# Attention weights of two heads side by side, retention decays moved to the values and the output, a third pair of banks in the last projection

## The chip, the cores and the metric

The kernel runs on one core of a Trainium2 chip. The metric is the device time of one execution in microseconds (us); the median of three executions of the kernel before is 3140.94 us (3136.82 to 3141.93). Below, PE is the matrix engine, DVE the vector engine, ACT the scalar engine, POOL the general engine, SP the queue that issues the DMAs.

## What is computed

Two layers of a block with four token mixers side by side, on 2048 tokens of width 1024 and 256 context tokens: a gated linear recurrence, a delta-rule memory (GDN), retention, and attention in a window. The change touches retention and attention. Cut to them:

```python
def retention_chunked(q, k, v, log_gamma, s0, with_out):   # per head, chunk by chunk
    s_new = s * c_dec + einsum('cd,ce->de', k_i * k_dec, v_i)
    att = einsum('id,jd->ij', q_i, k_i) * dmat
    o = einsum('cd,de->ce', q_i * q_dec, s) + einsum('ij,je->ie', att, v_i)

# attention: softmax over 256 context keys and a window of three blocks of 128 keys, then
#   y = P @ v, two query heads to each of two key-value heads, times a gate

y = concatenate([ya, yb, yr, yd]) @ w_out      # the projection at the end of each layer
x = x + gate * rmsnorm(y)
```

Retention runs forward and backward, so each decay exists for two directions.

## The kernel before

Tokens are cut into 18 tiles of 128 (two of context) and 9 blocks of two tiles. Each layer runs four stages:

- **A**: norms, and the projections for the recurrence and GDN.
- **B**: `ret_tile` and `gdn_tile` for every tile, with the projection for retention beside them as filler; the two scans `ret_scan` and `gdn_chain` begin here.
- **C**: the projection for attention, `swa_prep` and `swa_tile` (attention), and `ret_out` and `gdn_out`, which join what stage B left in DRAM with the scanned states.
- **D**: the projection with `w_out` (`proj`) and the norm and residual (`post`). In layer 0 it also prepares the next layer; in layer 1 (the **last projection**) it ends the program.

Python generators yield pieces of work, `weave` interleaves them, and this decides which PSUM buffer each piece takes. PSUM has eight banks of 128x512 f32: two `pd`, two `pg`, two `pm`, and `sc`, which is two banks in one tile. After that `Plan` lists the instructions with their dependencies, and sets a new order on every engine by the length of the chain behind each instruction, with a price for changes of shape on PE. So any edit moves instructions everywhere, but a bank is handed on in the order in which the program asked for it.

An f32 product stands in the trace as two MATMUL records, so four products show as x8. The products of the large projections are in f32r and show as one record each, and so do transposes.

The places of the change:

- `ret_tile` (stage B) per tile: q and k are rotated; `kd` holds k times the key decay of both directions (DVE); four products of `kd` (128 columns as weights) with 64 columns of v give the state increments `KV` (L145, tile `sc<-G`, 128x64). `qd` holds q times the query decay of both directions (POOL); four transposes turn q and k (L787), four more turn `qd` (L793), ACT copies both, and `qdT` goes to DRAM as `Qr`.
- `ret_scan`: the state S, forward in partitions 0 to 63 and backward in 64 to 127.
- `ret_out` (stage C) per tile: four products of `Qr` (128x128 weights) with 64 columns of S in one `pm` bank (L145, `pm<-U` 128\*128, 128x64), one DVE addition (L853), then the norm of each head.
- `swa_tile` (stage C): for each of four head steps the scores go to `sc`, the softmax runs on DVE and ACT, the weights are transposed in `pg` (L1470) and copied to `sPT` (ACT, L1471). After the second step of each half, the product with the values: for each of up to five key tiles two products, one for each key-value head, each with 64 columns of v as weights and 128 columns of `sPT`, into the two halves of a `pm` bank (`pm<-U` 128\*64, 128x128); then the gate (DVE, L1479). There are two such groups per tile.
- `proj` in the last projection: tile s = 0 of a block goes to the two `pd` banks, tile s = 1 to the two `pg` banks, 48 products of 512 columns each. `post` squares both banks on ACT (L1558), sums (L1560), takes the inverse root on POOL (L330) and scales both banks on DVE (L1571); a bank is free after its L1571. The input of a block (`h`) has two buffers, loaded and split by ACT, DVE and POOL (L1520 to L1524).

Of the kernel before, what the change touches and what calls it, by code (L numbers as in the profile page):

```python
# [16 lines left out]
NT = 18  # L17
# [6 lines left out]
PMAP = dict(x.split(":") for x in "ptk:0 ptv:h1 pt:0 pu:1 ptq:1 pm0:0 pm1:1 pc0:h0 pc1:h1 po:1 p3:1 rkv:h0 rpt:0 rpt2:0 rpo:h0 ch:h0".split())  # L24
# [45 lines left out]
    "C": ([("sqk", 384, 1), ("sks", 384, 1), ("srope", 256, 2), ("rota", 256, 1), ("rotb", 256, 1), ("sVc", 128, 2), ("sV", 128, 5),  # L70
           ("sqs", 512, 1), ("szt", 512, 1), ("szl", 512, 1), ("shs", 512, 1), ("roq", 512, 1), ("goq", 512, 1), ("goS", 512, 1),
           ("roS", 256, 1), ("roo", 256, 1), ("roz", 256, 1), ("rosq", 256, 1), ("goo", 256, 1), ("gosq", 256, 1), ("goz", 256, 1),
           ("roy", 256, 1), ("goy", 256, 1), ("sy", 256, 2), ("sPT", 640, 2), ("szb", 512, 2), ("sP", 640, 2)],
# [51 lines left out]
class Net:  # L125
# [134 lines left out]
    def setup(self):  # L260
# [33 lines left out]
        self.Qr = self.t(dp, [NT, 128, 512], "Qrd")  # L294
        self.KV = self.t(dp, [NT, 128, 256], "KVd")
        self.Sr = self.t(dp, [NT, 128, 256], "Srd")
# [411 lines left out]
    def ret_setup(self, sp):  # L708
# [20 lines left out]
        self.cdec = self.t(self.lp, [128, 4], "rcd")  # L729
        for d in range(2):  # L730
            nc.vector.tensor_scalar(self.qdec[:, :, d], lg[:, 4 * d:4 * d + 4], io[:, 2 * d:2 * d + 1], None, op0=MULT)
            nc.vector.tensor_scalar(self.kdec[:, :, d], lg[:, 4 * d:4 * d + 4], io[:, 2 * d + 1:2 * d + 2], None, op0=MULT)
            nc.vector.tensor_scalar(self.cdec[64 * d:64 * d + 64], lg[64 * d:64 * d + 64, 4 * d:4 * d + 4], 128.0, None, op0=MULT)
# [13 lines left out]
    def ret_tile(self, t, pa, pb, pp):  # L747

        nc = self.nc
# [18 lines left out]
        kd = self.t(pp, [128, 4, 2, 64], "rdd")  # L768
        nc.vector.tensor_tensor(kd, qk[:, 256:].rearrange("p (h e) -> p h e", h=4)[:, :, None].to_broadcast([128, 4, 2, 64]),
# [8 lines left out]
        self.st('K').dma_start(self.KV[t], kv)  # L778
# [35 lines left out]
    def ret_scan(self, lo, hi):  # L814
        nc = self.nc
        if lo == 0:
            self.rS = self.t(self.lp, [128, 4, 64], "rS", bufs=2)
            nc.vector.memset(self.rS, 0.0)
        fl = lambda a: a.rearrange("p h e -> p (h e)")
        for i in range(lo, hi):  # L820
# [3 lines left out]
            self.st('S').dma_start(self.Sr[tf, 0:64], fl(S)[0:64])  # L824
            self.st('S').dma_start(self.Sr[tb, 64:128], fl(S)[64:128])
# [3 lines left out]
            kv = self.t(self.lp, [128, 4, 64], "rsk", bufs=2)  # L829
            nc.sync.dma_start(fl(kv)[0:64], self.KV[tf, 0:64])  # L830
            nc.sync.dma_start(fl(kv)[64:128], self.KV[tb, 64:128])
            S2 = self.t(self.lp, [128, 4, 64], "rS", bufs=2)
            nc.vector.tensor_tensor(S2, S, self.cdec[:, :, None].to_broadcast([128, 4, 64]), op=MULT)
# [4 lines left out]
    def ret_out(self, t, pp):  # L838
# [3 lines left out]
        q = self.t(pp, [128, 512], "roq")  # L842
        nc.sync.dma_start(q, self.Qr[t])
        S = self.t(pp, [128, 256], "roS")
        nc.sync.dma_start(S, self.Sr[t])
# [578 lines left out]
    def swa_tile(self, t, qT, zb, pp):  # L1424
# [14 lines left out]
        y = self.t(pp, [128, 2, 128], "sy", bufs=2)  # L1439
# [23 lines left out]
        def second(hh, g):  # L1463
            p = P[hh, g]
            pT = PT[g] = self.t(pp, [128, 640], "sPT", bufs=2)
            for a in range(0, nk, 512):
# [4 lines left out]
                nc.scalar.copy(pT[:, a:a + w], pt[:, :w])  # L1471
# [8 lines left out]
            if hh:  # L1480
                self.st('s').dma_start(self.yT[t // 2, :, 6:8, s * 128:(s + 1) * 128], y)
            yield 1.3, 0
# [4 lines left out]
    def pass_d(self, pp):  # L1487
# [40 lines left out]
        outs = [0]  # L1528
# [512 lines left out]
```

## Time and profile before

| | us |
|---|---|
| median of three runs | 3140.94 |
| the profiled execution | 3140.24 |
| its span in the trace | 3138.5 |
| stage B of layer 0 and of layer 1, about | 400 to 960, 1990 to 2540 |
| stage C of layer 0 and of layer 1, about | 960 to 1400, 2540 to 2916 |
| last projection | 2916 to 3125 |
| after the last product | 3125 to 3138 |

In the trace's views a row of the timeline is a run of equal instructions: its start, its length up to the end of the last one, the engine, the line, the operation, the tile written and the tiles read, and how many. The time from one row's start to the next row's start is what the run took of PE's queue; the length itself also holds the time in which the last result runs out of the array, beside which the next run has begun. A bracket at a row's end gives the idle time ahead of it and what ended it.

### The profile page before, as it was taken

To read this page: it belongs to the slowest core of one execution; us is meant where nothing else is said; L and a number is where in the kernel's file an instruction comes from. 1 tells how busy PE (TensorE), PEld (TensorE's weight loads), DVE (VectorE), ACT (ScalarE), POOL (GpSimd) and SP (SyncE) were. 2 spreads that over 40 slices of the span, in tenths; PEclk is the share of its full clock that TensorE was granted. 3 is DMA by queue.
4 is the path that set the end of the run, shared out by engine and by line. 5 is a ranking of instruction groups with operands and counts; after the bars stand their busy time and mean duration, and the time that the engine had idled before them with its cause. 6 is when DMAs were issued, how large, how long until landed. Compare 5 with 4: busy or idle time off the path is not lost. (4 is left out here: it accounts for less than half of the span.)

```text
span 3138.5 us, 78206 instructions
## 1 busy us (share of the span) xinstructions
PE 2940.4 (94%) x31820; PEld 2497.3 (80%) x31820; DVE 1938.9 (62%) x4258; ACT 1334.3 (43%) x2930; POOL 1220.2 (39%) x1197
## 2 busy tenths in 40 slices
PE   4999979999999999979999998899999899999987
PEld 3999867778877888867789998678878688888766
DVE  4587777676665576653255787767666456767321
ACT  3466644444443344442134666444444424445211
POOL 2133345555542232334352333456555422323332
PEclk8999989999999999999999999999999999999998
DMA  7243465554456655375652435556444664544431
GB/s 275 95 173 134 166 168 150 167 153 118 134 180 187 199 163 162 122 264 196 197 202 106 162 144 162 161 150 176 141 140 120 220 198 139 171 152 142 153 122 68
DMA packets 410121, 504.69 MB, mean 161 GB/s; under 512 B 94056, under 2 KB 311560, under 8 KB 403104
## 3 DMA queue, kind: packets, MB, share of 16 engines
q1 hardware_dynamic: 409760, 499.68, 49.7%
q8 instruction: 250, 4.10, 0.5%
q14 instruction: 111, 0.91, 0.1%
HBM read 320.06 MB, written 179.50 MB: 159 GB/s over the span
## 5 line engine op out<-in xcount | busy, mean ns | idle before, releaser
L145 PE MATMUL pd<-w,h 128*128 128x512 f32 (+1 forms) x3408 | 984.4, 411 | 26.2 <-DVE U L1560 16.1
L145 PEld LDWEIGHTS pd<-w,h 128*128 128x128 f32 x3408 | 613.4, 192 | 158.6 <-ACT U L1558 18.5
L145 PE MATMUL pd<-h,w 128*128 128x256 f32 x3360 | 589.2, 294 | 1.1 <-DVE U L479 1.1
L145 PEld LDWEIGHTS pd<-h,w 128*128 128x128 f32 x3360 | 479.8, 193 | 10.6 <-issue 5.0
L330 POOL TENSOR_TENSOR U<-U,mh 128x4 f32<-128x4 f32 (+2 forms) x174 | 179.5, 1034 | 379.6 <-DVE U L329 361.2
L145 PE MATMUL pg<-h,w 128*128 128x256 f32 x1680 | 294.3, 294 | 4.7 <-DVE U L1571 3.6
L145 PE MATMUL pm<-U 128*64 128x128 f32 (+4 forms) x3280 | 249.4, 274 | 26.4 <-ACT U L1089 7.7
L145 PEld LDWEIGHTS pg<-h,w 128*128 128x128 f32 x1680 | 245.0, 191 | 9.9 <-DVE U L1571 3.8
L145 PEld LDWEIGHTS pm<-U 128*64 128x64 f32 (+2 forms) x3280 | 197.6, 143 | 68.4 <-issue 22.3
L145 PE MATMUL pg<-w,h 128*128 128x512 f32 x816 | 228.6, 394 | 1.3 <-DVE U L1571 1.3
L145 PEld LDWEIGHTS <-U 64*64 64x64 f16 x6512 | 153.2, 109 | 55.1 <-issue 45.4
L145 PE MATMUL pg<-U 64*64 64x64 f16 x6512 | 188.4, 195 | 1.2 <-DVE U L1031 1.1
L145 PEld LDWEIGHTS pg<-w,h 128*128 128x128 f32 x816 | 154.4, 190 | 38.8 <-issue 3.3
L1031 DVE TENSOR_TENSOR U<-pg,C 128x512 f16<-128x512 f32 x180 | 122.0, 684 | 64.3 <-PE pg L145 63.5
L625 DVE SCALAR_TENSOR_TENSOR U<-U 128x256 f32<-128x256 f32 x318 | 159.8, 552 | 1.1 <-POOL U L558 1.1
L1560 DVE TENSOR_TENSOR U<-U 128x1 f32<-128x1 f32 x34 | 7.7, 230 | 234.9 <-ACT U L1558 234.9
L1456 ACT ACTIVATE U<-sc,U 128x640 f32<-128x640 f32 (+2 forms) x136 | 104.2, 766 | 103.7 <-DVE U L1454 88.5
L1471 ACT COPY U<-pg 128x512 f32<-128x512 f32 (+2 forms) x248 | 100.7, 436 | 103.6 <-PE pg L1470 50.1
L1558 ACT ACTIVATE U<-pd 128x512 f32<-128x512 f32 x34 | 20.0, 594 | 276.7 <-PE pd L145 164.4
L1453 DVE TENSOR_REDUCE U<-sc 128x1 f32<-128x640 f32 (+2 forms) x136 | 106.2, 781 | 47.3 <-PE sc L145 45.7
L1046 DVE STREAM_TRANSPOSE U<-U 128x512 f16<-128x512 f16 x144 | 100.8, 703 | 45.8 <-ACT U L1042 45.3
L1042 ACT CAST U<-pg 128x512 f16<-128x512 f32 x144 | 84.0, 588 | 82.9 <-PE pg L145 77.9
(297 smaller groups left out, 6038.3 us busy)
## 6 DMA issues: line engine op xcount, KB each, us to landing
hTd<-h SPq DMA_DIRECT2D x18, 2048.0 KB, 6.7
h<-hTd SPq DMA_DIRECT2D x72, 512.0 KB, 5.6
h<-hTd SPq DMA_DIRECT2D x18, 2048.0 KB, 9.8
MCd<-U SPq DMA_DIRECT2D x72, 256.0 KB, 3.3
cMC<-MCd SPq DMA_DIRECT2D x140, 128.0 KB, 3.3
U<-yTd SPq DMA_DIRECT2D x34, 512.0 KB, 4.5
U<-in_w_in_dram SPq DMA_DIRECT2D x58, 256.0 KB, 3.9
hgd<-U SPq DMA_DIRECT2D x53, 256.0 KB, 2.5
```

The source lines that it names most:

```text
L145: self.nc.tensor.matmul(out, lhsT, rhs, start=start, stop=stop)
L330: nc.gpsimd.tensor_tensor(out, out, self.mh[:, :n], op=ALU.pow)
L625: nc.vector.scalar_tensor_tensor(z[:, i], xb[:, f, j:j + 256], cw[:, f, j:j + 1], z[:, i], op0=MULT, op1=ADD)
L1031: nc.vector.tensor_tensor(M, p1, lev(k), op=MULT)
L1042: nc.scalar.copy(Y, p2)
L1046: nc.vector.transpose(fl(YT), fl(Y))
L1453: nc.vector.tensor_reduce(m[:, h:h + 1], pv, axis=AX.X, op=MAXO)
L1456: nc.scalar.activation(p[:, :nk], pv, AF.Exp, bias=m[:, h:h + 1], accum_out=sums[:, h:h + 1])
L1471: nc.scalar.copy(pT[:, a:a + w], pt[:, :w])
L1558: nc.scalar.activation(x1[:, 512 * k:512 * k + 512], po[k], AF.Square, accum_out=ss[:, k:k + 1])
L1560: nc.vector.tensor_tensor(rs, ss[:, 0:1], ss[:, 1:2], op=ADD)
```

## The change

1. **Attention.** `sPT` is `[128, 5, 2, 128]` per key-value head and holds the transposed weights of both query heads side by side. The product with the values is made once per tile, with 256 moving columns; the gate is one DVE operation of 256 columns instead of two of 128.
2. **Retention.** The key decay goes on the values: `vd` is v for both directions, and the four products have 64 columns of k as weights and 128 columns of `vd`, in two column halves by head parity. `qd` (POOL), its four transposes (L793) and its copy (ACT) are gone, and the q half of `qkT` is stored. The state has the directions in the free dimension and the heads' parity in the partitions. `ret_out` makes four products of 64 rows with 128 columns, in two row halves, into two `pm` banks, one for each parity; then eight DVE operations of 64 columns multiply each head's part by its query decay and add it.
3. **Last projection.** In layer 1, every third tile from the second on takes the two banks of `sc`.

Tiles are resized for this (`sks`, `roq`, `sy`, `sPT`), which shifts the addresses of stage C.

```diff
-        kd = self.t(pp, [128, 4, 2, 64], "rdd")
-        nc.vector.tensor_tensor(kd, qk[:, 256:].rearrange("p (h e) -> p h e", h=4)[:, :, None].to_broadcast([128, 4, 2, 64]),
+        vd = self.t(pp, [128, 4, 2, 64], "rdd")
+        nc.vector.tensor_tensor(vd, v.rearrange("p (h e) -> p h e", h=4)[:, :, None].to_broadcast([128, 4, 2, 64]),
                                 self.kdec[:, :, :, None].to_broadcast([128, 4, 2, 64]), op=MULT)
...
+        pk4 = pkv[:, :256].rearrange("p (d a f) -> p d a f", d=2, a=2)
         for h in range(4):
-            self.mm(pkv[:, h * 64:(h + 1) * 64], kd[:, h].rearrange("p d e -> p (d e)"), v[:, h * 64:(h + 1) * 64])
+            self.mm(pk4[64 * (h % 2):64 * (h % 2) + 64, :, h // 2], qk[:, 256 + h * 64:256 + (h + 1) * 64], vd[:, h])
...
-        qd = self.t(pp, [128, 4, 2, 64], "rdd")
-        nc.gpsimd.tensor_tensor(qd, qk[:, :256].rearrange("p (h e) -> p h e", h=4)[:, :, None].to_broadcast([128, 4, 2, 64]),
-                                self.qdec[:, :, :, None].to_broadcast([128, 4, 2, 64]), op=MULT)
...
-        pt2 = self.slot("rpt2")
-        for h in range(4):
-            nc.tensor.transpose(pt2[:, h * 128:(h + 1) * 128], qd[:, h].rearrange("p d e -> p (d e)"), self.id)
-        qdT = self.t(pp, [128, 512], "rqkT", bufs=2)
-        nc.scalar.copy(qdT, pt2)
-        self.st('Q').dma_start(self.Qr[t], qdT)
-        yield 0.44, 2
+        self.st('Q').dma_start(self.Qr[t], qkT[:, :256])
...
-        po = self.pm()
-        for h in range(4):
-            self.mm(po[:, h * 64:(h + 1) * 64], q[:, h * 128:(h + 1) * 128], S[:, h * 64:(h + 1) * 64])
-        nc.vector.tensor_tensor(o0, po[:, :256], o0, op=ADD)
+        po = [self.pm()[:, :256].rearrange("p (a d f) -> p a d f", a=2, d=2) for _ in range(2)]
+        for a in range(2):
+            for par in range(2):
+                r = slice(64 * par, 64 * par + 64)
+                self.mm(po[par][:, a], q[r, a * 128:(a + 1) * 128], S[r, :, a])
         o4 = o0.rearrange("p (h e) -> p h e", h=4)
+        for d in range(2):
+            for h in range(4):
+                nc.vector.scalar_tensor_tensor(o4[:, h], po[h % 2][:, h // 2, d], self.qdec[:, h, d:d + 1], o4[:, h], op0=MULT, op1=ADD)
...
-            pT = PT[g] = self.t(pp, [128, 640], "sPT", bufs=2)
+            if hh == 0:
+                PT[g] = self.t(pp, [128, 5, 2, 128], "sPT", bufs=2)
...
-            if g == 0:
+            if g == 0 or hh == 0:
                 return
-            po = self.pm()[:, :128]
+            po = self.pm()[:, :256].rearrange("p (a n) -> p a n", a=2)
             for i, kt in enumerate(keys):
                 for k in range(2):
-                    self.mm(po[64 * k:64 * k + 64], self.V[kt][:, 64 * k:64 * k + 64], PT[k][:, i * 128:(i + 1) * 128], i == 0, i == len(keys) - 1)
-            nc.vector.tensor_tensor(y[:, hh], po, zb[:, hh, s * 128:(s + 1) * 128], op=MULT)
...
+                    self.mm(po[64 * k:64 * k + 64], self.V[kt][:, 64 * k:64 * k + 64], PT[k][:, i], i == 0, i == len(keys) - 1)
+            nc.vector.tensor_tensor(y, po, zb[:, :, s * 128:(s + 1) * 128], op=MULT)
...
-                        po = [self.pg() if s else self.pd() for _ in range(2)]
+                        n3[0] += 1
+                        if last and n3[0] % 3 == 2:
+                            po = self.sc().rearrange("p (a n) -> p a n", a=2)
+                            po = [po[:, 0], po[:, 1]]
+                        else:
+                            po = [self.pg() if s else self.pd() for _ in range(2)]
```

Where it moves instructions, three places on PE. The first is a change of blocks in the last projection; the number behind `pd`, `pg` or `sc` tells tiles apart, the number behind `h` the blocks' inputs. Before, both pairs of banks end together, and the next block follows in the same banks:

```order
L145 MATMUL pd_38652<-w_9_95,h_2277_38514 128x512
L145 MATMUL pd_38653<-w_9_95,h_2277_38514 128x512
L145 MATMUL pg_2285_38712<-w_9_95,h_2277_38514 128x512
L145 MATMUL pg_2286_38713<-w_9_95,h_2277_38514 128x512
L145 MATMUL pd_38781<-w_2_88,h_2282_38643 128x512 x3
L145 MATMUL pd_38782<-w_2_88,h_2282_38643 128x512 x3
```

Now, at the end of the fourth of the eight blocks:

```order
L145 MATMUL pd_38167<-w_9_95,h_2237_38030 128x512
L145 MATMUL pd_38168<-w_9_95,h_2237_38030 128x512
L145 MATMUL sc_38227<-w_7_93,h_2237_38030 128x512 x4
L145 MATMUL sc_38227<-w_8_94,h_2237_38030 128x512 x6
L145 MATMUL sc_38227<-w_9_95,h_2237_38030 128x512 x6
L145 MATMUL pg_2248_38355<-w_2_88,h_2241_38158 128x512
L145 MATMUL pd_38295<-w_2_88,h_2241_38158 128x512 x3
L145 MATMUL pd_38296<-w_2_88,h_2241_38158 128x512 x3
```

The `pd` pair ends 16 products before the `sc` pair, and the next block starts in `pg`, which is free, and in `pd`.

The second is a retention tile in stage B (`sc<-G` are its products, L793 and L787 or L786 its transposes, `pd<-w,h` the filler). Before:

```order
L145 MATMUL sc_3904<-G_233 128x128 x4
L793 MATMUL pm_301_6367<-C_96,G_233 128x128 x4
L145 MATMUL pd_6215<-w_9_95,h_171_3905 128x512
L1105 MATMUL pm_312_6560<-C_96,U_87 128x128 x4
L145 MATMUL pd_6215<-w_9_95,h_171_3905 128x512 x2
L940 MATMUL pm_303_6397<-C_96,U_87 128x128
L145 MATMUL sc_3904<-G_233 128x64 x4
```

Now:

```order
L145 MATMUL pg_416_8645<-U_87 64x64
L145 MATMUL sc_3904<-G_233 64x2x64 x4
L786 MATMUL pm_419_8730<-C_96,G_233 128x128 x4
L145 MATMUL pd_8630<-w_7_93,h_171_3905 128x512
L145 MATMUL pd_8953<-w_9_95,h_171_3905 128x512
```

The four products for `KV` have become 64x2x64 (64 weight columns, 128 moving), and the transposes of L793 have gone.

The third is in stage C of layer 1. Before, one group of the product with the values (64x128 x10), and `ret_out` (128x64 x4) in one piece:

```order
L145 MATMUL pm_2136_36677<-U_87 64x128 x10
L145 MATMUL sc_36763<-G_33307,F_33306 128x256
L145 MATMUL sc_36763<-G_33307,F_33306 128x384
L145 MATMUL sc_36763<-G_33307,F_33306 128x256
L145 MATMUL sc_36763<-G_33307,F_33306 128x384
L145 LDWEIGHTS bfid_98
L145 MATMUL sc_36763<-bfm_100,bfid_98 128x128
L145 LDWEIGHTS bfid_98
L145 MATMUL sc_36763<-bfm_100,bfid_98 128x128
L1470 MATMUL pg_2143_36735<-C_96,U_87 128x128 x3
L145 MATMUL pm_2150_36828<-U_87 128x64 x4
L1470 MATMUL pg_2143_36735<-C_96,U_87 128x128
```

Now:

```order
L145 MATMUL pm_1978_34829<-U_87 64x256 x10
L145 LDWEIGHTS bfid_98
L145 MATMUL sc_34842<-bfm_100,bfid_98 128x128
L145 LDWEIGHTS bfid_98
L145 MATMUL sc_34842<-bfm_100,bfid_98 128x128
L1196 MATMUL pm_1966_34740<-C_96,U_87 128x128
L1468 MATMUL pg_1980_34862<-C_96,U_87 128x128
L1196 MATMUL pm_1966_34740<-C_96,U_87 128x128
L1468 MATMUL pg_1980_34862<-C_96,U_87 128x128 x3
L1468 MATMUL pg_1981_34868<-C_96,U_87 128x128
L145 MATMUL pm_1984_34908<-U_87 128x128 x2
L145 MATMUL pm_1983_34907<-U_87 128x128 x2
```

The product stands once with 256 columns. `ret_out` stands as two products of one bank, so of one half of the rows, and then two of the other; 54 such pairs hold 108 of its 136 products, and 45 of the pairs have other work on both sides.

## Rows read from the trace of the kernel before

**Rows 1.** The page, parts 1 and 2: busy time; PE's granted clock in 40 slices.

```profile
PE 2940.4 (94%) x31820; PEld 2497.3 (80%) x31820; DVE 1938.9 (62%) x4258; ACT 1334.3 (43%) x2930; POOL 1220.2 (39%) x1197
PEclk8999989999999999999999999999999999999998
```

**Rows 2.** Busy time in stretches: last projection, middle of stage C, middle of stage B.

```profile
core 0: us, PE busy (x) PEld busy (x) DVE busy (x) ACT busy (x) POOL busy (x), PEclk, DMA share, GB/s
2916.30:3124.00 207.70, 188.42 (x782) 150.69 (x781) 51.68 (x77) 31.52 (x72) 67.37 (x44) 0.94 0.32 111
1040.00:1345.00 305.00, 299.51 (x2570) 265.24 (x2568) 213.85 (x603) 143.44 (x394) 91.06 (x115) 0.99 0.49 155
500.00:900.00 400.00, 397.60 (x7215) 316.27 (x7216) 266.76 (x508) 169.71 (x346) 213.10 (x189) 1.00 0.49 142
```

**Rows 3.** Timeline of the last projection, PE: start, two pairs, three block starts, end.

```profile
2916.34 0.73 PE L145 MATMUL pd<-w,h 128*128 128x512 f32 x2
...
2959.77 0.62 PE L145 MATMUL pd<-w,h 128*128 128x512 f32 x2
2960.22 0.62 PE L145 MATMUL pg<-w,h 128*128 128x512 f32 x2
...
2968.06 5.03 PE L145 MATMUL pd<-w,h 128*128 128x512 f32 x14 [2.69 <-DVE U L1560]
2972.93 3.36 PE L145 MATMUL pg<-w,h 128*128 128x512 f32 x14
...
2994.39 3.46 PE L145 MATMUL pd<-w,h 128*128 128x512 f32 x14 [2.69 <-DVE U L1560]
...
3101.13 6.41 PE L145 MATMUL pd<-w,h 128*128 128x512 f32 x20 [2.69 <-DVE U L1560]
...
3124.15 0.61 PE L145 MATMUL pg<-w,h 128*128 128x512 f32 x2
```

**Rows 4.** Waits of PE from 2850 us on: total, times, longest.

```profile
PE pd L145 <- DVE U L1560: 16.1, 6, 2.7
PE pd L145 <- DVE U L1571: 2.2, 1, 2.2
```

**Rows 5.** Timeline behind a block's last product: squares, first bank freed, next split.

```profile
2964.86 0.60 ACT L1558 ACTIVATE U<-pd 128x512 f32<-128x512 f32 x1 [22.52 <-PE pd L145]
...
2967.16 0.75 DVE L1571 SCALAR_TENSOR_TENSOR U<-pd,U,F 128x512 f32<-128x512 f32 x1 [0.66 <-POOL U L330]
...
2968.62 1.56 DVE L1524 TENSOR_TENSOR h<-U,h 128x512 fp32r<-128x512 f32 x1
```

**Rows 6.** Timeline, PE, at narrow products and transposes in stages C and B.

```profile
1348.89 1.31 PE L145 MATMUL pm<-U 128*64 128x128 f32 x20
1350.13 1.22 PE L145 MATMUL pd<-h,w 128*128 128x256 f32 x8
...
1273.32 1.00 PE L145 MATMUL pm<-U 128*128 128x64 f32 x8
1274.16 0.39 PE L1470 MATMUL pg<-C,U 128*128 128x128 f32 x2
1274.48 0.43 PE L145 MATMUL pm<-U 128*64 128x128 f32 x2
1274.85 0.38 PE L145 MATMUL pd<-h,w 128*128 128x256 f32 x1
...
561.38 0.71 PE L145 MATMUL sc<-G 64*128 64x128 f32 x8
562.02 0.66 PE L793 MATMUL pm<-C,G 128*128 128x128 f32 x4
562.43 0.48 PE L145 MATMUL pd<-w,h 128*128 128x512 f32 x1
...
611.17 0.48 PE L145 MATMUL sc<-G 64*128 64x128 f32 x2
611.59 0.66 PE L793 MATMUL pm<-C,G 128*128 128x128 f32 x4
```

**Rows 7.** Products with 256 f32 columns: busy and mean of the form; one run.

```profile
L145 PE MATMUL sc<-U 128*128 128x256 f32 x256 | 79.0, 390 | 6.6 <-ACT U L1242 5.8 <-DVE U L1230 0.5
201.12 0.60 PE L145 MATMUL sc<-U 128*128 128x256 f32 x2
```

**Rows 8.** DVE from a `pm` bank: min/median/max ns; last, who waited for L853.

```profile
L1479 DVE TENSOR_TENSOR U<-pm,U x68: 274/290/294, 999.7 to 2939.7; 128x128 f32<-128x128 f32 x68
L853 DVE TENSOR_TENSOR U<-pm,U x34: 408/422/426, 966.9 to 2860.8; 128x256 f32<-128x256 f32 x34
  PE pm L145: 4.3, 2
```

More of the change, by code (lines that the diff above doesn't have):

```diff
@@ L23 @@
 OWN = 1
-PMAP = dict(x.split(":") for x in "ptk:0 ptv:h1 pt:0 pu:1 ptq:1 pm0:0 pm1:1 pc0:h0 pc1:h1 po:1 p3:1 rkv:h0 rpt:0 rpt2:0 rpo:h0 ch:h0".split())
+PMAP = dict(x.split(":") for x in "ptk:0 ptv:h1 pt:0 pu:1 ptq:1 pm0:0 pm1:1 pc0:h0 pc1:h1 po:1 p3:1 rkv:h0 rpt:0 rpo:h0 ch:h0".split())
 PMAP.update(x.split(":") for x in ''.split())
@@ L293, in setup @@
         self.Qg = self.t(dp, [NT, 128, 512], "Qgd")
-        self.Qr = self.t(dp, [NT, 128, 512], "Qrd")
-        self.KV = self.t(dp, [NT, 128, 256], "KVd")
-        self.Sr = self.t(dp, [NT, 128, 256], "Srd")
+        self.Qr = self.t(dp, [NT, 128, 256], "Qrd")
+        self.KV = self.t(dp, [NT, 2, 128, 128], "KVd")
+        self.Sr = self.t(dp, [NT, 2, 128, 128], "Srd")
         self.Og = self.t(dp, [NT, 128, 256], "Ogd")
@@ L816, in ret_scan @@
         if lo == 0:
-            self.rS = self.t(self.lp, [128, 4, 64], "rS", bufs=2)
+            self.rS = self.t(self.lp, [128, 2, 2, 64], "rS", bufs=2)
             nc.vector.memset(self.rS, 0.0)
-        fl = lambda a: a.rearrange("p h e -> p (h e)")
+        fl = lambda a: a.rearrange("p a e -> p (a e)")
         for i in range(lo, hi):
@@ L828, in ret_scan @@
                 break
[L829 to L833, printed above, removed]
+            kv = self.t(self.lp, [128, 2, 2, 64], "rsk", bufs=2)
+            nc.sync.dma_start(fl(kv[:, 0]), self.KV[tf, 0])
+            nc.sync.dma_start(fl(kv[:, 1]), self.KV[tb, 1])
+            S2 = self.t(self.lp, [128, 2, 2, 64], "rS", bufs=2)
+            nc.vector.tensor_tensor(S2, S, self.cdec[:, :, :, None].to_broadcast([128, 2, 2, 64]), op=MULT)
             nc.vector.tensor_tensor(S2, S2, kv, op=ADD)
@@ L841, in ret_out @@
         s = t % 2
-        q = self.t(pp, [128, 512], "roq")
+        q = self.t(pp, [128, 256], "roq")
         nc.sync.dma_start(q, self.Qr[t])
-        S = self.t(pp, [128, 256], "roS")
-        nc.sync.dma_start(S, self.Sr[t])
+        S = self.t(pp, [128, 2, 2, 64], "roS")
+        nc.sync.dma_start(S.rearrange("p d a f -> p d (a f)"), self.Sr[t].rearrange("d p n -> p d n"))
         o0 = self.t(pp, [128, 256], "roo")
@@ L1438, in swa_tile @@
         rc = self.t(pp, [128, 4], "src", bufs=2)
-        y = self.t(pp, [128, 2, 128], "sy", bufs=2)
+        y = self.t(pp, [128, 2, 128], "sy")
         P, PT = {}, {}
@@ L1470, in second @@
                     nc.tensor.transpose(pt[:, i * 128:(i + 1) * 128], p[:, a + i * 128:a + (i + 1) * 128], self.id)
-                nc.scalar.copy(pT[:, a:a + w], pt[:, :w])
+                nc.scalar.copy(PT[g][:, a // 128:(a + w) // 128, hh], pt[:, :w].rearrange("p (i n) -> p i n", n=128))
             yield 0.55, 0.3
-            if g == 0:
+            if g == 0 or hh == 0:
                 return
-            po = self.pm()[:, :128]
+            po = self.pm()[:, :256].rearrange("p (a n) -> p a n", a=2)
             for i, kt in enumerate(keys):
                 for k in range(2):
-                    self.mm(po[64 * k:64 * k + 64], self.V[kt][:, 64 * k:64 * k + 64], PT[k][:, i * 128:(i + 1) * 128], i == 0, i == len(keys) - 1)
-            nc.vector.tensor_tensor(y[:, hh], po, zb[:, hh, s * 128:(s + 1) * 128], op=MULT)
-            if hh:
-                self.st('s').dma_start(self.yT[t // 2, :, 6:8, s * 128:(s + 1) * 128], y)
-            yield 1.3, 0
+                    self.mm(po[64 * k:64 * k + 64], self.V[kt][:, 64 * k:64 * k + 64], PT[k][:, i], i == 0, i == len(keys) - 1)
+            nc.vector.tensor_tensor(y, po, zb[:, :, s * 128:(s + 1) * 128], op=MULT)
+            self.st('s').dma_start(self.yT[t // 2, :, 6:8, s * 128:(s + 1) * 128], y)
+            yield 2.2, 0
         return [(first(hh, g), second(hh, g)) for hh in range(2) for g in range(2)]
@@ L1526, in loads @@
                 yield 0, 1
-        outs = [0]
+        outs, n3 = [0], [0]
         def proj():
```

17 lines of the change are left out of this document (9 added, 8 removed).

## The prediction, made before the changed kernel ran

> **What bounds the kernel now.** I read the page's busy shares first: PE is busy 94% of the span, DVE 62%, ACT 43%, POOL 39% [rows 1]. A busy share hides where the limit changes, so the stretches come next: in the middle of stages B and C PE is busy 99% and 98% of the time at nearly full clock, while DVE is at 67% and 70% [rows 2]. There the program is as long as PE's queue, and an edit is worth what it takes out of that queue. The last projection is different: PE is busy for 188 of 208 us and the granted clock is 0.94 [rows 2], so it loses time twice. The third view, the timeline, shows how. Two runs of two products start 0.45 us apart, so a product takes 0.2265 us [rows 3]; 16 tiles of 48 products are 768 × 0.2265 = 174 us, but from 2916.34 to the end at 3124.6 (the last run of two starts at 3124.15) are 208 [rows 3]. The 34 us go at the seven changes of block: from one to the next are 26.3 us (2968.06 to 2994.39) instead of 96 × 0.2265 = 21.7 [rows 3]. PE waits 2.69 us at six of them and 2.2 at one [rows 3, 4], because both pairs of banks end together and the first bank is free only when `post` has squared and scaled it: 2964.86 to 2967.91 [rows 5]. Behind the wait the clock is often at its lower level of 1.2 GHz for a while: 14 products take 4.9 us to the next row's start, 0.35 each [rows 3].
>
> **What narrow forms cost in PE's queue.** All by the time to the next row's start [rows 6]. Eight records with 128 weight columns and 64 moving: 0.84. Four transposes: 0.41. Twenty records of 64 weight columns and 128 moving, in alternating halves: 1.24; one such product alone (two records): 0.37. So a further pair of products, one in each half, costs (1.24 − 0.37)/4 = 0.22. Eight records of 64 rows, in alternating halves: 0.65; one product alone: 0.42. Going over to a narrow form also costs ahead of it: two transposes before one take 0.32 instead of 0.21, so 0.11.
>
> **The last projection: −29 us.** With `sc` as third pair one pair is always free at a change of block, and the new order starts the next block in it. Where a pair is taken again soonest it ended 16 products, 3.6 us, before; the first bank is free 3.05 us after the squares begin, the second 0.74 later [rows 5], so a few tenths of a microsecond remain. The input of the next block is next late: its first split ends at 2970.18, 5.3 us after the last block's squares began [rows 5], and the two blocks whose buffer was freed last start some 42 products, 9.5 us, behind that. All 34 us would be gone if nothing waited; I leave 5 for tight changes and one or two stretches at the lower clock (range 22 to 33). The tail behind the last product stays.
>
> **Retention in stage B: −23 us in the queue.** The four transposes of L793 go: 34 tiles × 0.41 = −14. The four products for `KV` become two pairs of half width: 0.37 + 0.22 = 0.59 instead of 0.84, 36 tiles × −0.25 = −9. The POOL product, ACT copy and half of the `Qr` store that go with L793 had PE's 99% above them and bring nothing on the path; `vd` replaces `kd` at the same size. `KV` and `Sr` go through SP in as many transfers as before.
>
> **`ret_out` in stage C: +7 us in the queue.** In alternating halves the four products would cost 0.65 instead of 0.84. But the order puts the two products of one bank together, which share their rows: 0.42 for the first and 2 × 0.11 for the second, 0.64; for both banks 1.28. With 45 of 54 pairs standing alone, 45 × 0.64 + 11.5 tiles × 0.65 = 36 us against 34 × 0.84 = 29.
>
> **The product with the values: −6 us.** The moving columns stay as many, and columns set the pace here: a record with 256 f32 columns starts 0.21 behind the one before it (0.60 for two, 0.39 for one) [rows 7], twice the 0.11 of 128. A tile in one piece then costs 0.37 + 0.21 for the first pair and 4 × 0.44 for the others, 2.3 instead of 2 × 1.24; 34 × −0.18 = −6. Half the weight loads and half the gates on DVE (68 of 0.29 become 34 of 0.42 [rows 8]) go, but both lie beside other work.
>
> The Trainium skill, "TensorE: Matmul & The Clock Gate", part 3, "What overlaps and what doesn't", says that a weight load runs beside a matmul only where the two use different rows of the array. The product uses all 128 rows in both halves, so by that rule its 640 saved loads would come out of the queue, by the same page's 64 columns/1.2 GHz an estimated 34 us. The trace speaks against it: 20 loads of 53 ns and 10 pairs of 0.107 us in sequence would be 2.1 us, and the row has 1.24 [rows 6].
>
> **Turns: +6 us.** Counted over the two programs' PE order, the runs of these narrow products go from 132 to 185; 53 × 0.11 = +6, beyond what the prices above hold.
>
> **Waits in stage C: +5 us.** `ret_out` now holds both `pm` banks until eight DVE operations are done. From 128 to 256 columns DVE goes from 0.290 to 0.422 us [rows 8], so 64 columns are 0.22; the nearest row of the same operation, 512 columns with a scalar from PSUM, is 0.75 [rows 5], which leaves 0.29 for 64. Eight are 1.8 to 2.3 us, against 0.42 of L853. Behind them wait all who use `pm`: the transposes of `swa_prep`, the product, `gdn_out` and `gdn_chain`. L853 made PE wait 4.3 us in all [rows 8]; PE has the projection for cover, and I take 5 more, between 0 and 20. DVE gets 34 × 1.6 − 5 = 49 us more over two stages of some 400, from 70% to 76%, still under PE.
>
> **Sum.** −29 − 23 + 7 − 6 + 6 + 5 = −40. The profiled execution took 3140.2 us (span 3138.5, 1.7 around it), 0.7 under the median: 3140.2 − 40 = **3100 us**. By the bounds of the terms this case reaches from 3084 to 3114.
>
> **The rivals.**
> - *Loads set the pace of the product*, not columns. Then one product for both heads costs what one head did: 34 × (2.3 − 1.24) = 36 us more gain, **3064**. For it: at 128 columns the rows can't tell the two apart. Against: rows 7. This is the skill's rule above, as a mechanism. 5%.
> - *Only the last projection pays.* Reordering everything costs as much in turns and waits as the transposes and `KV` give: 3140 − 29, and up to 10 us more waiting in stage C: **3111 to 3121**. For it: no piece but L793 is taken away outright. Against: 99% PE in stage B, where nothing else is near its limit. 18%.
> - *The seams stay.* The split of the next input, on ACT, DVE and POOL among two tiles' `post`, comes late, PE's strict order hangs on it, and the clock still falls: **3129**. For it: that split follows the squares closely even now [rows 5]. Against: 9.5 us of cover. 8%.
> - *Slower: `ret_out` shuts both `pm` banks.* Products out of the array, handover and eight operations are some 2.5 us per tile; with no other work ready 34 × 2.5 = 85 us, **3185**. It decides from 40/34 = 1.2 us uncovered per tile on. For it: L853 was already waited for, and both banks go at once. Against: in stage C PE was busy 98%, so cover is there nearly always. 7%.
>
> **How the numbers follow.** Forecast 62%, rivals 5, 18, 8 and 7. The range of 8 in 10 holds the forecast, the second rival and a part of the third: 3070 to 3127; the first and the last lie outside. A measurement of this kernel tells about 0.2%, 6 us, from no change. Faster by more than that: forecast, the first two rivals and half of the third, 0.89; within it 0.05; slower 0.06.
>
> **What would show it.** In the last projection: PE waits under 0.5 us at changes of block, granted clock near 1, 174 to 186 us from first to last product. In stage B: no L793, runs of `sc<-G` 128\*64 at about 0.6 us. In stage C: records of 256 columns about 0.21 apart within a half; pairs of `ret_out` at 0.6; eight DVE rows of 0.22 to 0.29; little PE wait for them. Stage B shorter by 8 to 12 us per layer, stage C by no more than 5. Wrong would be: 0.11 between records of 256 columns (first rival), stage B no shorter (second), waits over 2 us at changes of block for `h` (third), or stage C longer by 20 us per layer (last).

## The result, and the profile after

The changed kernel takes **3099.6 us** (median of four runs, 3092.84 to 3101.53) against 3140.6 of the kernel before (four runs, 3136.82 to 3141.93): a ratio of 0.9868, 95% interval 0.9853 to 0.9883, or 41 us less, where 3100 and 40 less were forecast. The profiled execution is the fastest of its four (span 3090.9 us), so the stages below add up to 47.6 us, not to 41.

The page of the changed kernel, busy time and granted clock in 40 slices. PE's share is as in [rows 1], but its busy time is 29 us less, DVE's 38 more:

```profile
PE 2911.2 (94%) x31044; PEld 2432.0 (79%) x31044; DVE 1977.3 (64%) x4462; ACT 1318.0 (43%) x2896; POOL 1189.0 (38%) x1163
PEclk8999989999999999999999999899999999999999
```

Cut into stages, the busy time of the kernel before: stage B of the first layer, stage C with the first projection (to the next layer's first transpose of L406), then B and C of the second layer, and the last projection. Stage B ends with the last f16 product of the delta rule:

```profile
core 0: us, PE busy (x) PEld busy (x) DVE busy (x) ACT busy (x) POOL busy (x), PEclk, DMA share, GB/s
324.50:945.40 620.90, 592.44 (x9377) 475.99 (x9375) 429.38 (x835) 284.89 (x581) 320.04 (x280) 0.98 0.53 155
945.40:1618.30 672.90, 640.19 (x4694) 530.31 (x4688) 362.75 (x936) 243.13 (x635) 218.38 (x218) 0.97 0.57 187
1890.20:2493.10 602.90, 574.02 (x9239) 467.58 (x9239) 413.45 (x822) 278.61 (x570) 312.72 (x274) 0.97 0.53 155
2493.10:2916.30 423.20, 395.98 (x3456) 345.19 (x3448) 273.81 (x744) 179.34 (x484) 120.76 (x147) 0.96 0.53 168
2916.30:3138.50 222.20, 189.18 (x784) 151.00 (x782) 54.94 (x85) 33.95 (x80) 73.11 (x48) 0.93 0.31 108
```

The same stages of the changed kernel:

```profile
324.40:930.60 606.20, 575.11 (x9291) 460.23 (x9289) 422.44 (x835) 274.48 (x561) 298.74 (x261) 0.97 0.53 155
930.60:1607.30 676.70, 647.32 (x4380) 518.93 (x4373) 386.44 (x1043) 244.10 (x634) 220.05 (x217) 0.98 0.56 182
1879.70:2467.90 588.20, 558.08 (x9166) 448.52 (x9166) 417.88 (x825) 268.52 (x553) 298.97 (x258) 0.97 0.54 158
2467.90:2898.60 430.70, 403.37 (x3148) 331.72 (x3140) 289.77 (x833) 179.02 (x481) 121.05 (x147) 0.96 0.51 155
2898.60:3090.90 192.30, 177.95 (x789) 145.51 (x788) 56.55 (x89) 36.35 (x84) 73.88 (x48) 0.98 0.36 129
```

Stage B is 14.7 us shorter in each layer (29.4 together), stage C 3.8 and 7.5 longer (11.3), the last projection 29.9 shorter. In stage C DVE's busy time rises by 23.7 and 16.0 us, and PE's by 7 in each layer. The border between B and C moves with the order, though: the variant with the last projection alone, below, changes nothing in either, and there stage B is 6 and 7 us longer than before (626.7 and 609.6) and stage C 2 and 7 shorter. So the split into 29.4 and 11.3 is uncertain by such amounts; the sum of both stages, 18.1 us less, is the firmer figure (that variant's sum is 4.0 us more).

The last projection, PE's timeline of the changed kernel: the start, the only wait in it (for the split of the first input), and a stretch at a change of block.

```profile
2898.55 1.19 PE L145 MATMUL pd<-w,h 128*128 128x512 f32 x4
2900.47 0.50 PE L145 MATMUL pd<-w,h 128*128 128x512 f32 x1 [0.72 <-DVE h L1521]
...
2951.54 0.62 PE L145 MATMUL pg<-w,h 128*128 128x512 f32 x2
2951.99 5.15 PE L145 MATMUL sc<-w,h 128*128 128x512 f32 x22
2956.98 0.62 PE L145 MATMUL pg<-w,h 128*128 128x512 f32 x2
```

The waits of [rows 4] are gone: 22 products into `sc` follow at 4.99/22 = 0.227 each with no row of waiting. From the first to the end of the last product are 178.5 us, PE is busy for 177.78 of them at a granted clock of 1.00, against 0.94 in [rows 2]:

```profile
2898.50:3077.00 178.50, 177.78 (x790) 145.57 (x788) 53.38 (x82) 34.26 (x77) 68.17 (x44) 1.00 0.38 134
```

The narrow forms of the changed kernel, PE's timeline (each with the row that starts next): the product for two heads as a whole and one of its ten products alone (two records), two pairs of `ret_out`, one `KV`.

```profile
1110.91 2.38 PE L145 MATMUL pm<-U 128*64 128x256 f32 x20
1113.22 0.50 PE L145 MATMUL pd<-h,w 128*128 128x256 f32 x2
...
1222.23 0.65 PE L145 MATMUL pm<-U 128*64 128x256 f32 x2
1222.81 0.44 PE L1196 MATMUL pm<-C,U 128*128 128x128 f32 x2
...
1147.81 0.71 PE L145 MATMUL pm<-U 64*128 64x128 f32 x4
1148.45 0.39 PE L145 MATMUL pd<-h,w 128*128 128x256 f32 x1
...
1149.81 0.71 PE L145 MATMUL pm<-U 64*128 64x128 f32 x4
1150.45 0.98 PE L145 MATMUL pd<-h,w 128*128 128x256 f32 x6
...
1999.18 0.66 PE L145 MATMUL sc<-G 128*64 128x128 f32 x8
1999.77 0.50 PE L145 MATMUL pd<-w,h 128*128 128x512 f32 x1
```

To the next start these are the forecast prices: 2.31 for the product (2.3), 0.58 for its first product (0.37 + 0.21 for the first pair, from [rows 6, 7]), 0.64 for half a `ret_out` (0.64), 0.59 for `KV` (0.59). On DVE, a timeline row and a row of the groups: the eight operations of `ret_out` in sequence, and the time of one.

```profile
1153.41 1.62 DVE L851 SCALAR_TENSOR_TENSOR U<-pm,ab,U 128x64 f32<-128x64 f32 x8
...
L851 DVE SCALAR_TENSOR_TENSOR U<-pm,ab,U x272: 262/276/286, 948.1 to 2848.0; 128x64 f32<-128x64 f32 x136
```

One takes 0.276 us, within the forecast's 0.22 to 0.29; eight overlap at their ends and take 1.62, less than the 1.8 to 2.3 put down for them.

PE's waits, total, times and longest, first one of the kernel before, then two of the changed kernel:

```profile
PE sc L145 <- ACT U L1456: 3.2, 6, 2.0
```

```profile
PE sc L145 <- ACT U L1453: 15.5, 17, 3.4
PE pd L145 <- DVE U L479: 8.1, 7, 3.6
```

L1453 (L1456 before) is the exponential of the scores: PE waits for the `sc` bank that it still reads. L479 is a gate on DVE that empties a `pd` bank; before, PE waited 1.6 us for it. What the exponential itself waits for is seen from ACT, in the idle time ahead of it, first of before, then of the changed kernel: it is DVE's scaled maximum.

```profile
  DVE U L1454: 88.5, 66
```

```profile
  DVE U L1451: 109.0, 61
```

### The profile page after: what moved, and what is told of

Its sections match the earlier page's. It is cut to its first block, busy times and chain, and to the rows that moved or that the text cites. A ratio compares the mean times of both kernels' runs of the same rounds, so it can differ in the third digit from the quotient of the medians.

```text
span 3090.9 us, 76692 instructions
## 1 busy us (share of the span) xinstructions
PE 2911.2 (94%) x31044; PEld 2432.0 (79%) x31044; DVE 1977.3 (64%) x4462; ACT 1318.0 (43%) x2896; POOL 1189.0 (38%) x1163
## 5 line engine op out<-in xcount | busy, mean ns | idle before, releaser
L145 PE MATMUL pd<-w,h 128*128 128x512 f32 (+1 forms) x3312 | 931.5, 408 | 13.9 <-DVE U L479 5.9
L145 PEld LDWEIGHTS pd<-w,h 128*128 128x128 f32 x3312 | 596.2, 191 | 146.8 <-issue 11.6
L145 PE MATMUL pm<-U 64*64 64x128 f32 (+4 forms) x2640 | 251.2, 299 | 10.2 <-ACT U L1469 2.9
L145 PEld LDWEIGHTS pm<-U 64*64 64x64 f32 (+3 forms) x2640 | 167.9, 142 | 74.0 <-issue 20.8
L145 PEld LDWEIGHTS <-U 64*64 64x64 f16 x6624 | 164.5, 109 | 63.0 <-issue 52.9
L145 PE MATMUL pg<-U 64*64 64x64 f16 x6624 | 202.8, 195 | 4.7 <-DVE U L1028 2.6
L145 PE MATMUL pg<-w,h 128*128 128x512 f32 x672 | 180.4, 390 | 2.7 <-ACT h L1518 2.6
L1453 ACT ACTIVATE U<-sc,U 128x640 f32<-128x640 f32 (+2 forms) x136 | 104.2, 767 | 120.7 <-DVE U L1451 109.0
L145 PEld LDWEIGHTS pg<-w,h 128*128 128x128 f32 x672 | 125.9, 188 | 32.5 <-ACT h L1518 3.6
L145 PE MATMUL sc<-G,F 128*128 128x256 f32 (+1 forms) x528 | 109.8, 324 | 15.7 <-ACT U L1453 15.5
```

The source lines that it names most:

```text
L145: self.nc.tensor.matmul(out, lhsT, rhs, start=start, stop=stop)
L1453: nc.scalar.activation(p[:, :nk], pv, AF.Exp, bias=m[:, h:h + 1], accum_out=sums[:, h:h + 1])
```

## The experiments

Eleven variants ran. "us under" is one minus the ratio, times the median of the kernel before on that chip (3141 for the changed kernel, 3145 to 3146 for the others). B+C is the time of these two stages of both layers in the profiled run, 2319.9 before: the cut between them moves by several us with the order, as the first variant shows, which changes nothing there (2323.9), so their sum says more than either alone.

| kernel | ratio, 95% interval | us under | B+C | C, first layer | C, second layer |
|---|---|---|---|---|---|
| before | 1 | 0 | 2319.9 | 672.9 | 423.2 |
| changed | 0.9868 (0.9853 to 0.9883) | 41 | 2301.8 | 676.7 | 430.7 |
| last projection alone | 0.9906 (0.9892 to 0.9919) | 30 | 2323.9 | 671.0 | 416.6 |
| retention alone | 0.9987 (0.9977 to 0.9996) | 4 | 2318.2 | 698.8 | 421.8 |
| attention alone | 0.9999 (0.9990 to 1.0008) | 0 | 2316.6 | 672.4 | 414.9 |
| retention and last projection | 0.9877 (0.9864 to 0.9891) | 39 | 2319.1 | 699.4 | 418.9 |
| retention, wide operations | 0.9958 (0.9945 to 0.9971) | 13 | 2311.3 | 685.1 | 430.5 |
| retention, tied | 0.9955 (0.9940 to 0.9969) | 14 | 2310.7 | 683.6 | 424.0 |
| retention, last projection, tied | 0.9841 (0.9828 to 0.9855) | 50 | 2300.1 | 684.6 | 420.0 |
| **changed, tied** | **0.9781 (0.9764 to 0.9798)** | **69** | 2280.1 | 670.1 | 414.9 |
| changed, tied, 128 columns | 0.9787 (0.9771 to 0.9803) | 67 | 2286.6 | 672.3 | 419.1 |

Not in the table: the changed kernel with wide operations (0.9850, interval 0.9832 to 0.9867, 47 under) and with wide operations and tie (0.9786, 0.9772 to 0.9800, 67 under).

### The parts alone

The last projection alone, as in the change:

```diff
-                        po = [self.pg() if s else self.pd() for _ in range(2)]
+                        n3[0] += 1
+                        if last and n3[0] % 3 == 2:
+                            po = self.sc().rearrange("p (a n) -> p a n", a=2)
+                            po = [po[:, 0], po[:, 1]]
+                        else:
+                            po = [self.pg() if s else self.pd() for _ in range(2)]
```

> The kernel before with one part of the change alone: the third pair of banks (`sc`) in the last projection. Theory (the term of the prediction, with what the changed kernel's trace shows, last scores to last product 32.9 us shorter): -29 to -33 us, so 3107 to 3112, with no PE wait of over 0.7 us at the seven changes of block and 175 to 181 us from first to last product. Rival, the gain in the changed kernel's last projection is partly owed to the other parts (stage C ending with its queue in another order): under 24 us, 3117 or more.

Measured: 30 us under, 3114.6. The last projection takes 179.5 us from first to last product (178.5 in the changed kernel), at clock 1.00 and without a row of waiting. The term stands by itself and owes nothing to the other parts.

The retention alone: the lines of the change from `PMAP` to `ret_out`, of which the core is

```diff
-            self.mm(pkv[:, h * 64:(h + 1) * 64], kd[:, h].rearrange("p d e -> p (d e)"), v[:, h * 64:(h + 1) * 64])
+            self.mm(pk4[64 * (h % 2):64 * (h % 2) + 64, :, h // 2], qk[:, 256 + h * 64:256 + (h + 1) * 64], vd[:, h])
...
-            nc.tensor.transpose(pt2[:, h * 128:(h + 1) * 128], qd[:, h].rearrange("p d e -> p (d e)"), self.id)
...
-        nc.vector.tensor_tensor(o0, po[:, :256], o0, op=ADD)
+                nc.vector.scalar_tensor_tensor(o4[:, h], po[h % 2][:, h // 2, d], self.qdec[:, h, d:d + 1], o4[:, h], op0=MULT, op1=ADD)
```

> The kernel before with the retention part alone (decays moved to the values and to the output of `ret_out`, no scaled and transposed queries). Theory: stage B 22 to 27 us shorter over the two layers, stage C longer by 7 for the products of `ret_out`, 2 to 4 for turns and 5 for waits: -5 to -13 us, 3128 to 3136. Rival one, what stage C loses is owed to the product with the values and `ret_out` costs only its products: -16 to -20, 3121 to 3125. Rival two, `ret_out` is the whole loss in stage C (14 to 19 us): -5 to -12 with stage C longer by 14 or more; the stretches of the scores then are 6 and 12 us longer, as in the changed kernel.

Measured: 4 us under. Stage B gives its 26 us (606.0 and 591.6 against 620.9 and 602.9), and the first layer's stage C takes 25.9 back. Its stretches, with the second layer's:

```profile
929.30:1628.10 698.80, 657.05 (x4712) 536.75 (x4706) 388.81 (x1062) 245.32 (x637) 222.59 (x217) 0.97 0.55 178
2491.10:2912.90 421.80, 396.64 (x3440) 339.59 (x3434) 291.37 (x847) 179.34 (x479) 122.94 (x147) 0.97 0.51 158
```

PE's waits of transposes for a `pm` bank in both layers, first before, then here:

```profile
PE pm L1415 <- DVE U L1184: 6.2, 3, 3.5
...
PE pm L1407 <- DVE U L1184: 2.7, 1, 2.7
```

```profile
PE pm L1412 <- DVE U L1181: 8.2, 5, 2.7
PE pm L1412 <- DVE U L1451: 8.1, 3, 2.9
...
PE pm L1196 <- DVE U L851: 4.8, 2, 3.8
```

These are transposes of `swa_prep` (L1412, L1404; before, L1415 and L1407) and `gdn_out` (L1196) that want a `pm` bank; L1181 (before, L1184) and L851 are the DVE operations by which `gdn_out` and `ret_out` empty theirs. L1451, the scaled maximum, touches no `pm` bank: each time it ended 0.12 us after an L1181, so the first two lines are most likely one and the same wait, 16.3 us in eight times where the kernel before has 8.9 in four. The wait for L851 is about what [rows 8] has for L853, 4.3. In the first layer alone these are 8.6 and 3.8 us, where the kernel before has 2.3 and 2.3: 8 more, less than a third of what its stage C lost. PE's busy time there rises by 17 us with 18 records more; what grew in both layers, from start to start, are `ret_out` (28.7 to 37.7 us) and the unchanged product with the values (95.7 to 105.6). Rival two has its loss, but in the first layer only, and its other sign by half: scores of 256 columns and masks take 71.4 us, where the kernel before has 63.7 and the changed one 79.2.

The attention part alone:

```diff
-                    self.mm(po[64 * k:64 * k + 64], self.V[kt][:, 64 * k:64 * k + 64], PT[k][:, i * 128:(i + 1) * 128], i == 0, i == len(keys) - 1)
-            nc.vector.tensor_tensor(y[:, hh], po, zb[:, hh, s * 128:(s + 1) * 128], op=MULT)
+                    self.mm(po[64 * k:64 * k + 64], self.V[kt][:, 64 * k:64 * k + 64], PT[k][:, i], i == 0, i == len(keys) - 1)
+            nc.vector.tensor_tensor(y, po, zb[:, :, s * 128:(s + 1) * 128], op=MULT)
```

> The kernel before with the attention part alone (one product with the values for two heads; the last projection and the retention as before). Theory, columns set the pace: the product's records fall by 6 us or more in sum, the scores wait a little more for their weights: -8 to +3 us, 3133 to 3144. Rival, loads set the pace of the product: -30 to -40, 3101 to 3111.

Measured: 0 (3 slower to 3 faster). The gain of 34 us by saved weight loads is not there, though the product's records fall from 95.7 to 88.9 us.

The change without the attention part, the same lines undone:

```diff
...
-            po = self.pm()[:, :256].rearrange("p (a n) -> p a n", a=2)
+            po = self.pm()[:, :128]
...
```

> The changed kernel with the attention part undone: one product with the values for each head, as before. Theory: the product for two heads is worth 6 us, so 3103 to 3108. Rival, the wide product costs stage C more than it gives (the wait of the scores for the exponential, 15.5 us in the changed kernel against 3.2, is its doing): 3090 to 3099.

Measured: 39 under, against 41 of the changed kernel; the intervals overlap, so the 3 us that the part is worth here can't be told from nothing. Its rival is out. But the first layer's stage C is 699.4 us without the part and 676.7 with it: there the part gives back most of what the retention had cost, which its records alone can't do. The wait of `swa_prep` for `gdn_out`'s bank, 16.9 us without the part, is 0.2 with it; against that the wait for the exponential goes from 6.3 to 15.5.

### The split of `ret_out`

The eight operations hold both banks for 1.62 us. In the wide form two multiplications empty the banks, and four additions follow in SBUF:

```diff
...
-        for d in range(2):
-            for h in range(4):
-                nc.vector.scalar_tensor_tensor(o4[:, h], po[h % 2][:, h // 2, d], self.qdec[:, h, d:d + 1], o4[:, h], op0=MULT, op1=ADD)
...
+        for par in range(2):
+            nc.vector.tensor_tensor(tm[par], po[par].rearrange("p a d f -> p (a d) f"), self.qdec[:, par, :, None].to_broadcast([128, 4, 64]), op=MULT)
+        for par in range(2):
+            for d in range(2):
+                nc.vector.tensor_tensor(o5[:, par], tm[par][:, d::2], o5[:, par], op=ADD)
```

> The changed kernel with `ret_out`'s eight DVE operations of 64 columns turned into two multiplications of 256 columns with a broadcast decay, which read the two banks, and four additions of 128 in SBUF. In the changed kernel the eight take 1.62 us in sequence and hold both banks as long; the two should take 0.7 to 0.8. Theory, the hold of the banks is part of stage C's loss: 4 to 10 us faster than the changed kernel, so 45 to 51 under the kernel before. Rival, the banks are free soon enough and DVE's total time counts (six operations of some 1.6 us are no less): the same as the changed kernel, 41 +- 5 under the kernel before.

> The retention part alone, with the wide multiplications. With the eight narrow operations the retention alone gave only 4 us: stage B 28 us shorter, stage C 25 longer, nearly all of it in the first layer, where PE waited for DVE behind `ret_out` (L1412 for L1451, L1196 for L851). Theory, the eight operations (held banks and DVE's queue) are that loss: stage C of the first layer 10 to 20 us shorter than with the narrow ones, 14 to 24 under the kernel before. Rival, the loss lies in the products' places and in PE's order: 0 to 8 under the kernel before.

Measured: in the changed kernel 47 under against 41, intervals that overlap: not told apart from no change. With the retention alone it gives 9 us (13 against 4): the first layer's stage C falls by 13.7 us, as the theory has it, but the second's, with the last projection, is 2.6 longer. So the eight operations are a part of that loss, not all of it: the wait for `gdn_out`'s bank falls from 16.3 to 5.5 us, and PE now waits 10.0 for the two wide ones (L852). Whether it is the hold of the banks or the place in DVE's queue, this doesn't part.

The tie gives the four products each other's conditions in the planner, so that they start together and the halves of rows stand side by side:

```diff
...
+        for names in self.net.pairs:
+            ks = {k for n in names for k in users[n] if self.eng[k] == PE}
+            ext = set().union(*(pre[k] for k in ks)) - ks
+            for k in ks:
+                pre[k] |= ext
```

> The changed kernel where the planner lets `ret_out`'s four products start only when both banks can be taken, so that their row halves stand together in PE's queue. In the changed kernel the 272 records take 39.2 us to the next row's start, 0.64 for a run of four records (one bank alone) and 0.65 for a run of eight. Theory: 34 tiles at 0.65 are 22 us, so 13 to 17 us go, less some 3 for the later start: 51 to 58 under the kernel before. Rival, the wait for the second bank and the moved rows around it take it back: the same as the changed kernel, 41 +- 5 under the kernel before.

Measured: 69 under, more than the theory asked: **3076.3 us**, 27 less than the changed kernel by the ratios (their intervals leave 20 to 35) and the best of all. PE's timeline shows what the tie buys: all four products (eight records) in the time that two took alone.

```profile
1043.56 0.72 PE L145 MATMUL pm<-U 64*128 64x128 f32 x8
1044.21 0.74 PE L145 MATMUL pd<-w,h 128*128 128x512 f32 x2
```

Added up over all 272 records, from one's start to the next one's, `ret_out` takes 23.3 us instead of 39.2. Behind that the scores get on earlier: their products of 256 columns and their masks, added up alike, take 67.0 us instead of 79.2 (the wait for the exponential, which is in them, falls from 15.5 to 9.0). These are 28 us in sum, more than the 22 by which stage C is shorter in the profiled runs: other records take some back (the transposes of L1470 2.7). The 16 of `ret_out` follow from the tie; that the rest does is likely, not shown. The stretches of stage C:

```profile
928.80:1598.90 670.10, 644.26 (x4382) 513.79 (x4377) 382.50 (x1045) 243.28 (x637) 218.60 (x217) 0.98 0.57 184
2460.70:2875.60 414.90, 392.09 (x3136) 324.47 (x3129) 293.27 (x830) 179.06 (x478) 123.70 (x147) 0.95 0.53 160
```

> Both edits together. Theory: the sum of the two, 55 to 66 us under the kernel before. Rival: no more than the better one of the two.

Measured: 67 under, as the tie alone: the wide operations add nothing to it, as the rival has it.

> The retention part alone, with `ret_out`'s four products tied to both banks. Alone and untied it gave 4 us. Theory, the split of the products (0.64 for two of four) and what waits behind them in stage C is what the part lost: as in the changed kernel 16 us for the products and some 10 behind them, so 20 to 32 under the kernel before. Rival, the tie pays only with the two-head product, which leaves more banks free: 2 to 12 under the kernel before.

Measured: 14 under (10 to 19), between the two expectations and nearer the rival. The tie is worth 10 us without the attention part (`ret_out`'s records fall by 13), and 27 with it.

### What the product for two heads is worth

The tied kernel without the attention part (one product for each head, as in the diff above):

> Retention and last projection with the tie, and one product with the values for each head as before: what is the two-head product worth beside the tied kernel, which was 69 us under the kernel before? Theory, the 6 to 10 us of its records: 58 to 64 under the kernel before. Rival one, it is worth more, since it takes half as many `pm` banks and so keeps `ret_out` from waiting: 45 to 55 under. Rival two, nothing: 66 to 72 under.

Measured: 50 under, 19 less than with the part: the size of rival one, though it isn't `ret_out` that waits. `swa_prep`'s transposes (L1414 here) wait for `gdn_out`'s bank (L1183) as they did with the retention alone; in the tied kernel with the part this wait is not in the list. PE's wait, and the stretches of stage C:

```profile
PE pm L1414 <- DVE U L1183: 18.3, 8, 5.2
```

```profile
929.70:1614.30 684.60, 645.60 (x4708) 527.35 (x4701) 386.12 (x1062) 244.71 (x637) 222.62 (x217) 0.98 0.56 180
2475.50:2895.50 420.00, 392.21 (x3427) 336.93 (x3420) 290.76 (x843) 177.08 (x475) 123.27 (x147) 0.97 0.51 158
```

The last one parts the columns and loads from the bank: one bank and one place for both heads, as in the change, but products of 128 columns, each with its own weight load.

```diff
...
-            for i, kt in enumerate(keys):
-                for k in range(2):
-                    self.mm(po[64 * k:64 * k + 64], self.V[kt][:, 64 * k:64 * k + 64], PT[k][:, i], i == 0, i == len(keys) - 1)
+            for a in range(2):
+                for i, kt in enumerate(keys):
+                    for k in range(2):
+                        self.mm(po[64 * k:64 * k + 64, a], self.V[kt][:, 64 * k:64 * k + 64], PT[k][:, i, a], i == 0, i == len(keys) - 1)
```

> The tied kernel with the product for two heads in one bank, at one place, but each weight load followed by products of 128 columns again, 640 more loads and as many columns. Theory, columns set the pace: two runs of 20 records at 1.24 us less one start, 2.3 to 2.5 us a tile as with 256 columns; the same as the tied kernel within 6 us, 63 to 72 under the kernel before. Rival, loads set the pace: 34 us slower, 30 to 40 under the kernel before.

Measured: 67 under, as the tied kernel with 256 columns. Forty records of 128 columns take 2.34 us to the next row's start, twenty of 256 took 2.31:

```profile
1118.12 2.40 PE L145 MATMUL pm<-U 128*64 128x128 f32 x40
1120.46 0.85 PE L145 MATMUL sc<-G,F 128*128 128x256 f32 x4
```

So 640 weight loads more cost nothing that can be measured, and this kernel, with one `pm` bank for both heads, is 17 us faster than the one with two banks, run on the same chip (intervals 0.9771 to 0.9803 and 0.9828 to 0.9855). So neither columns nor loads make the part's worth. What is left is the bank, which the vanished wait of 18.3 us speaks for, and what changed along with it: one place for both heads' product, one gate on DVE instead of two, and tiles at other addresses. No run parts these.

By the Trainium skill, "TensorE: Matmul & The Clock Gate", part 3, "What overlaps and what doesn't", these loads would not have run beside products that use the same rows. The row of forty speaks against it: loads and products together take 2.34 us to the next start, where the products with half the loads take 2.31. Nor is it owed to the halves of columns: in the changed kernel's last projection, where loads and products alike use all rows and columns, loads are busy for 145.57 and products for 177.78 of 178.50 us (its row stands in the section on the result), so nearly all of the loads' time lies beside products.

## Why the prediction was right, and where its steps were not

The total was hit within 1 us, and that is partly luck: the errors of the terms below cancel, and 41 us is uncertain by 5 either way. The term of the last projection, three quarters of the gain, was not.

- *The last projection −29*: right. 29.9 in the stage, 30 alone (25 to 34). The waits are gone, the clock is 1.00, and 178.5 us are within the 174 to 186 named. Seams that stay (3129) are out.
- *Retention in stage B −23*: a little small. The stage gave 29.4, or 14.7 in each layer where 8 to 12 were named. Added up from start to start, the transposes of L793 took 17.5 us before, not 14: the 0.41 of [rows 6] is the time ahead of a product of full width, and 21 of the groups of four stood ahead of narrow ones, at 0.53 to 0.59; the products for `KV` went from 37.8 (69.3 for all products of that shape, less the 31.5 that the others take in the changed kernel) to 30.7, so −7 for −9 forecast. The rest, 5 us, is not assigned, and is no more than the border of the stage moves.
- *`ret_out` +7*: mis-sized. It was 10.5 (28.7 to 39.2 for all records). The prices per run were right; 45 runs of one bank and 11 of both stand in the trace, but a few were longer than 0.64, up to 1.36. The larger fault is that the split was taken as given. Undone, it is worth 27 us beside the attention part and 10 without it, 16 and 13 of them in the products.
- *The product with the values −6*: right in the rows, wrong as a reason. Its records take 86.0 us instead of 95.7 (2.7 of the 9.7 are idle time), and the tile of 2.31 us is the 2.3 that was named. Yet alone it gave 0, and beside the tie it gave 17 to 19, the 17 with as many columns and weight loads as before. The sum left out what the part does to the banks: the retention makes each tile take three `pm` tiles for `ret_out` instead of two, the attention part one for the product instead of two.
- *Turns +6*: a wrong count. Counted alike in the order of both programs, the runs of the product with the values fall from 95 to 52, those of `ret_out` rise from 38 to 58, and those of `KV`, with the other products that had its shape before, from 73 to 75; in all they fall from 206 to 185. The 132 and 185 come out only if that last group is left out before (133) and counted after. At 0.11 each the term would have been −2, and the forecast 3092.
- *Waits +5*: right in size at most, wrong in place. Stage C is 11.3 us longer, where 7 − 6 + 6 + 5 gave 12, by a border that is uncertain by 7. For L851, named as the cause, PE hardly waits in the changed kernel (0.6 us, its weight loads, where [rows 8] has 4.3 for L853); it waits for the exponential (15.5 us against 3.2), and that for the maximum from DVE (88.5 to 109.0 us of ACT's idle time). DVE's 40 us more in stage C are not enough to explain it: in the tied kernel DVE is as busy there (675.8 us, 676.2 in the changed one), yet ACT's idle time is 81.8 us and PE's wait 9.0. The waits for a `pm` bank that were foreseen came in the kernels without the attention part.
- *The rivals*: loads as pace (3064) fell twice, with 0 of the part alone and with forty records in 2.34 us. Of the slower one, both banks shut, the retention alone shows something at a third of the price: 26 us in the first layer, not 85, of which 3.8 stand as waits for L851 (2.3 for L853 before); the wide operations, which free the banks sooner, gave 9 us back.
- *Only the last projection pays* (3111 to 3121) was nearer than its 18% let it look: retention alone is 4 us and attention alone 0. Alone the three parts make 34, the last projection with the retention 39, all together 41; with intervals of 3 to 5 us, a joint effect isn't shown in the untied kernel. With the tie it is: 17 to 19 us for the attention part.
- *The range*: the two ranges that the terms give (22 to 33, 0 to 20) make 3091 to 3122, not 3084 to 3114; the result lies in both.

What stays open: why the retention alone loses 26 us in the first layer's stage C and nothing in the second's. The planner's order differs between them; no run here separates that. Nor what of the attention part's worth beside the tie is the bank's.

## What to carry to other kernels

Where an order of work decides, a part that gives nothing alone can be what makes another pay: run each part alone and each part left out before calling one useless, and count how many buffers a tile takes before and after, not only how long its work is. Count runs and turns of both kernels with one rule. When halves of the array can run side by side, see in the order that they do; here a tie between four products gave 27 us.

## What the runs showed of the hardware

- Two products of 64 rows in one half alone cost 0.64 us to the next start, four in alternating halves 0.65: the second pair is free if the halves alternate.
- Weight loads run beside products although both use all 128 rows. With 64 weight columns: forty records of 128 columns with forty loads in 2.34 us, twenty of 256 columns with twenty loads in 2.31. With all 128 weight columns: loads busy for 145.57 us and products for 177.78 in one stretch of 178.50.
- Eight DVE operations of 64 columns from PSUM take 0.276 us each, but 1.62 in sequence, 0.2 per operation.
